# Strassen sums of the FFN's second product put together by adding transfers

## The chip, the cores and the metric

The kernel runs on one core of one Trainium2 chip. The metric is the device time of one execution in microseconds (us). The kernel before took 2555.97 us, the median of three runs (2553.58 to 2556.56). A change of 0.2%, about 5.1 us, is roughly what a measurement of this kernel can tell from none.

The engines have short names here: PE is TensorE, PEld its weight loads, DVE is VectorE, ACT is ScalarE, POOL is GpSimd and SP is SyncE, which issues transfers.

## The reference

Four layers, each a token mixer (latent attention, retention, gated linear attention, latent attention) and then an FFN, on 512 tokens of width 1024, all in float32. Only the FFN is touched:

```python
D_MODEL, SEQ, DEPTH = 1024, 512, 4
FFN_HIDDEN = 2816

def swiglu_ffn(x, w_in, w_out):
    gate, up = jnp.split(x @ w_in, 2, axis=-1)
    return (jax.nn.silu(gate) * up) @ w_out

# per layer, after the mixer:
x = layer_norm(DEEPNORM_ALPHA * x + swiglu_ffn(x, ffn_w_in[i], ffn_w_out[i]), ln_g[i, 1], ln_b[i, 1])
```

## The kernel before

Every product of two float32 matrices is made of three matmuls. An operand is split into a high part, rounded by an ACT cast, and a low part, the rest, subtracted on DVE (`split`, L100 to L103); `mm3` (L124) then multiplies high by high, high by low and low by high. Weights take this path: a transfer issued by SP fills a buffer `wraw` (three of them, 512 KB each), ACT writes `whi`, DVE writes `wlo` (six of each), and PE reads these two. A slot of `whi` and `wlo` comes free when the matmuls on it are done.

**The FFN.** The hidden width is cut into 22 blocks of 128, counted by f. For each f there are two projections, gate and up, of 24 matmuls each over `xh` and `xl` (tokens in 512 columns). ACT takes the silu of the gate, DVE multiplies it with the up part. For the blocks 0 to 15 the second product, with `w_out`, is done by a Strassen scheme. Two blocks, f even and f odd, make a pair. The product of the pair goes into one tile `ft` with room for seven 128x256 factors. Two of its four halves come with the even block and two with the odd one (DVE, L322). Then POOL makes the remaining factors with four adds and subtracts (L325 to L328), ACT casts all seven to `fh` and DVE subtracts the rest into `fl`. There is a single `ft`, so the next pair's first multiply waits until `fl` is done.

**The seven products.** Two pairs, four blocks of f, make a group, and `ffn_out` returns seven steps for it: p1, p5, p6, p2, p3, p7, p4. The four quarters of the weights' rows are called by the diff b11, b12, b21 and b22 (a 128 x 2 x 512 tile, 512 KB, each). Each step splits one tile of weights and runs 12 matmuls on it. The results are added from PSUM to the residual `xt` or to a tile `u`. The steps of a group run after the projections of the four blocks that follow it, two after each of the first three and one after the last (from f = 16 on they are spread over the blocks to 21). There are four groups per layer, 16 in all.

**The weights' sums before.** p1 loads b11 into a `wraw` buffer and b12 and b22 into two of the three buffers `wt`; p6 loads b21 into the third. Four DVE subtractions (L387) per group overwrite these buffers in place: b12-b11 for p5, b22 minus that for p6, b21 minus that for p4, b22-b12 for p7.

**The order.** A scheduler places the instructions: each engine runs its own list strictly in order, and an instruction whose semaphores are not up holds back all that stand behind it on its engine. This goes for SP and POOL too, whose lists also hold the transfers that they issue.

Of the kernel before, what the change touches and what calls it, by code (L numbers as in the profile page):

```python
# [9 lines left out]
F32 = mybir.dt.float32  # L10
# [3 lines left out]
ALU = mybir.AluOpType  # L14
AX = mybir.AxisListType

P = 128
# [5 lines left out]
ALPHA = (2.0 * DEPTH) ** 0.25  # L23
# [27 lines left out]
class Trunk:  # L51
# [121 lines left out]
        nc.sync.dma_start(self.bb, self.ins["ln_b"][i, k].partition_broadcast(P))  # L173
        self.stats = [self.small(12, "lnst") for _ in range(NT)]

    def acc(self, t, half, ps, coef, last):
        nc = self.nc
        x = self.xt[t][:, half * 512 : half * 512 + 512]
        if coef is None:
            nc.vector.tensor_tensor(x, ps, x, op=ALU.add)  # L180
        else:
            nc.vector.scalar_tensor_tensor(x, x, coef, ps, op0=ALU.mult, op1=ALU.add)
        if last:
            nc.vector.bn_stats(self.stats[t][:, half * 6 : half * 6 + 6], x)

# [110 lines left out]
    def ffn(self, l, out=None):  # L296
        nc = self.nc
        w_in, w_out = self.ins["ffn_w_in"][l], self.ins["ffn_w_out"][l]
        ns = 16
        self.fact, hs = {}, {}  # L300
        self.u = self.b((P, 2, 512), tag="u", name="u")
        half = lambda a: a.rearrange("p (a n) -> p a n", a=2)

        def evac(f, pg, pu):
            s = self.b()
            nc.scalar.activation(s, pg, AF.Silu)
            if f >= ns:
                if f < NF - 2:
                    if f % 2 == 0:
                        self.hp = self.b((P, 2, 512), F32R, "hh", "fh"), self.b((P, 2, 512), F32R, "hl", "fh")  # L310
                    h = tuple(x[:, f % 2, :] for x in self.hp)
                else:
                    h = self.bpair()
                nc.vector.tensor_tensor(s, pu, s, op=ALU.mult)
                self.split(h[0], h[1], s)
                hs[f] = h
                return
            if f % 2 == 0:
                self.ft = self.b((P, 7, 256), tag="ft", name="ft")
            ft = self.ft  # L320

            nc.vector.tensor_tensor(ft[:, 2:4, :] if f % 2 else ft[:, 1::-1, :], half(pu), half(s), op=ALU.mult)  # L322
            if f % 2:
                tt = nc.gpsimd.tensor_tensor
                tt(ft[:, 4, :], ft[:, 0, :], ft[:, 3, :], op=ALU.add)  # L325
                tt(ft[:, 5, :], ft[:, 4, :], ft[:, 1, :], op=ALU.subtract)
                tt(ft[:, 0, :], ft[:, 1, :], ft[:, 0, :], op=ALU.subtract)
                tt(ft[:, 6, :], ft[:, 2, :], ft[:, 5, :], op=ALU.subtract)  # L328
                h = self.b((P, 7, 256), F32R, "fh", "fh"), self.b((P, 7, 256), F32R, "fl", "fh")
                self.split(h[0], h[1], ft)  # L330
                self.fact[f // 2] = h

        nh = 3
        first = []
        for f in range(nh):
            wg = self.wcols(w_in, 0, KT, f * P, P)
            wu = self.wcols(w_in, 0, KT, F + f * P, P)
            first.append((wg, self.ps()))
            first.append((wu, self.ps()))
        for t0 in (0, 2):  # L340
            for n, (w2, ps) in enumerate(first):
                self.proj_f(w2, ps[:, t0 * P : (t0 + 2) * P], KT, lambda k: self.xm(k, t0, t0 + 2))
                if n % 2:
                    self.flush(2 + n // 2)
        for f in range(nh):
            evac(f, first[2 * f][1], first[2 * f + 1][1])
        rot = False
        todo = []
        for f in range(nh, NF):
            if f == nh + 1:  # L350
                rot = self.before(l + 1, nc.vector)
            if f == NF - 4 and rot:
                self.rope_sin()
            wg = self.wcols(w_in, 0, KT, f * P, P)
            pg = self.ps()
            self.proj_f(wg, pg, KT, self.xm)
            wu = self.wcols(w_in, 0, KT, F + f * P, P)
            pu = self.ps()
            self.proj_f(wu, pu, KT, self.xm)
            evac(f, pg, pu)  # L360
            if 4 <= f < ns + 4 and f % 4 == 0:
                c = f // 4 - 1
                todo = self.ffn_out(w_out, 2 * c, 2, c == 0)
            left = (4 - f % 4) if f < ns else NF - f
            for _ in range(-(-len(todo) // left) if todo else 0):
                todo.pop(0)()
        for tt in range(2):
            for hf, c in ((0, 1), (1, 0), (1, 1)):
                x = self.xt[2 * hf + tt][:, c * 512 : c * 512 + 512]
                nc.vector.tensor_tensor(x, x, self.u[:, tt, :], op=ALU.add)  # L370
        self.ln_begin(l, 1)
        st = lambda f, t: tuple(x[:, t * P : (t + 1) * P] for x in hs[ns + f])
        self.out_proj(st, w_out[ns * P :], NF - ns, None, True, out)

    def ffn_out(self, w, g0, n, begin):


        nc = self.nc
        rows = w[2 * g0 * P : 2 * (g0 + n) * P, :].rearrange("(g a p) c -> a p g c", a=2, p=P)
        B = {}  # L380

        def load(name, a, c, t):
            nc.sync.dma_start(t, rows[a][:, :, c * 512 : c * 512 + 512])
            B[name] = t

        wt = lambda: self.b((P, n, 512), name="wt", tag="t")
        sub = lambda to, x, y: nc.vector.tensor_tensor(B[to], B[x], B[y], op=ALU.subtract)  # L387

        def product(name, slot, to, u=None):

            hi, lo = self.wsplit(B[name], n, 512)
            ps = [self.ps() for _ in range(2)]
            for tt in range(2):
                for i in range(n):
                    s2 = tuple(x[:, slot, tt * P : (tt + 1) * P] for x in self.fact[g0 + i])
                    self.mm3(ps[tt], s2, (hi[:, i, :], lo[:, i, :]), i == 0, i == n - 1)
                for hf, c, first in to:
                    self.acc(2 * hf + tt, c, ps[tt], ALPHA if first else None, False)
                if u is not None:
                    x = self.u[:, tt, :]  # L400
                    if u:
                        nc.scalar.copy(x, ps[tt])
                    else:
                        nc.vector.tensor_tensor(x, ps[tt], x, op=ALU.add)

        s3, a11, a12, a22, s1, s2, s4 = range(7)

        def p1():
            load("1", 0, 0, self.wp.tile([P, n, 512], F32, tag="wraw", name="wraw", bufs=self.nraw))
            load("2", 0, 1, wt())  # L410
            load("3", 1, 1, wt())
            product("1", a11, [(0, 0, begin)], begin)

        def p5():
            sub("1", "2", "1")
            product("1", s1, [(0, 1, begin), (1, 1, begin)])

        def p6():
            sub("1", "3", "1")
            load("4", 1, 0, wt())  # L420
            product("1", s2, [], False)

        def p2():
            product("4", a12, [(0, 0, False)])

        def p3():
            sub("4", "4", "1")
            sub("2", "3", "2")
            product("3", s4, [(0, 1, False)])

        def p7():
            product("2", s3, [(1, 0, begin), (1, 1, False)])

        def p4():
            product("4", a22, [(1, 0, False)])

        return [p1, p5, p6, p2, p3, p7, p4]

    def load_x(self, x):

# [856 lines left out]
```

## Time and profile before

| | before |
|---|---|
| median of three runs | 2555.97 us |
| the profiled execution | 2556.05 us |
| its span, first to last instruction | 2554.2 us |
| PE busy in the span | 2524.5 us (99%) |
| DVE busy | 1776.7 us (70%) |
| ACT busy | 976.8 us (38%) |
| POOL busy | 212.4 us (8%) |
| mean granted clock of TensorE | 0.998 |
| DMA | 232.36 MB, 29.9% of the 16 engines' time |

The profile is of one execution, 1.9 us longer than its span and within 0.1 us of the median. A busy time is the time in which an engine has at least one instruction running. PE's matmuls overlap, so a matmul that is listed with 389 ns can follow the one before it after 226 ns: the rate is read from counts in a stretch, not from durations. The FFN stages lie at about 212 to 590, 1036 to 1372, 1640 to 1970 and 2190 to 2554 us.

### The profile page before, as it was taken

Reading aid. Unit: us, or ns where it says so; the run is one execution under the profiler, and the core shown is the slowest. Engines: PE = TensorE matmul, PEld = TensorE weight load, DVE = VectorE, ACT = ScalarE, POOL = GpSimd, SP = SyncE. Lnnn points to the kernel's source line nnn. Section 1 sums busy time; section 2 is a strip of 40 time slices with the busy share of each in tenths; the row PEclk is TensorE's granted clock in tenths of the full one; section 3 lists DMA queues with packets and bytes.
Section 4 is the critical chain, followed back from the end, with each engine's and each line's share of the span. In section 5 each row is a group of like instructions: output and inputs, shape, how many; then the busy total and the mean of one; then the engine's idle time right before and its main releaser. Section 6 shows DMA issues by size and latency. Waiting matters only on the chain.

```text
span 2554.2 us, 32600 instructions
## 1 busy us (share of the span) xinstructions
PE 2524.5 (99%) x12804; PEld 2147.2 (84%) x12804; DVE 1776.7 (70%) x2980; ACT 976.8 (38%) x1405; POOL 212.4 (8%) x279
## 2 busy tenths in 40 slices
PE   8999999999999999999999999999999999999998
PEld 7788888888888888988888899988888788988887
DVE  6887766658655647666657878966657686666656
ACT  4653333323342323333332665233332564233331
POOL 3000111000101101111100000011100200011101
PEclk9999999999999999999999999999999999999999
DMA  4213333323222333333333322333332311333331
GB/s 149 75 42 95 99 102 105 99 83 100 76 90 66 95 96 99 99 99 99 107 99 82 91 74 75 112 99 99 99 91 79 91 58 57 109 99 99 99 91 58
DMA packets 294714, 232.36 MB, mean 91 GB/s; under 512 B 21120, under 2 KB 244480, under 8 KB 294560
## 3 DMA queue, kind: packets, MB, share of 16 engines
q1 hardware_dynamic: 294560, 230.28, 29.9%
q8 instruction: 100, 1.64, 0.3%
q14 instruction: 54, 0.44, 0.1%
HBM read 228.15 MB, written 2.10 MB: 90 GB/s over the span
## 4 chain that ended last, share of the span: by engine, by line
PE 93%; DVE 3%; ACT 2%; DMA 1%; issue 1%; POOL 1%; SPq 0%; DVEq 0%; ACTq 0%; POOLq 0%
PE ps L126 30%; PE ps L127 30%; PE ps L128 30%; PE tp L659 1%; PE tp L156 1%; DVE wlo L102 1%; PE ps L640 1%; PE ps L639 0%; ACT whi L101 0%; DMA wraw<-in_mla_w_ukv 0%; DMA wraw<-in_mla_w_down 0%; DMA wraw<-in_ret_w_in 0%; ACT bh L101 0%; ACT b L549 0%; PE tp L903 0%
## 5 line engine op out<-in xcount | busy, mean ns | idle before, releaser
L101 ACT CAST whi<-wraw 128x1024 fp32r<-128x1024 f32 (+3 forms) x398 | 411.9, 1040 | 699.0 <-PE ps L127 234.1
L126 PE MATMUL ps<-xh,whi 128*128 128x512 f32 (+1 forms) x1792 | 656.8, 367 | 0.0
L127 PE MATMUL ps<-xl,whi 128*128 128x512 f32 (+1 forms) x1792 | 656.5, 366 | 0.1
L128 PE MATMUL ps<-xh,wlo 128*128 128x512 f32 (+1 forms) x1792 | 656.4, 366 | 0.0
L102 DVE TENSOR_TENSOR wlo<-wraw,whi 128x1024 fp32r<-128x1024 f32 (+3 forms) x398 | 487.6, 1234 | 212.5 <-ACT whi L101 205.1
L128 PEld LDWEIGHTS ps<-xh,wlo 128*128 128x128 f32 x1792 | 337.9, 189 | 55.0
L127 PEld LDWEIGHTS ps<-xl,whi 128*128 128x128 f32 x1792 | 337.9, 189 | 54.9 <-DVE lnx L139 0.3
L126 PEld LDWEIGHTS ps<-xh,whi 128*128 128x128 f32 x1792 | 337.6, 189 | 55.3 <-issue 0.4
L126 PE MATMUL ps<-whi,xh 128*128 128x512 f32 (+3 forms) x752 | 264.5, 352 | 0.7 <-ACT xh L101 0.7
L128 PE MATMUL ps<-whi,xl 128*128 128x512 f32 (+3 forms) x752 | 262.6, 349 | 2.3 <-DVE xl L102 2.3
L127 PE MATMUL ps<-wlo,xh 128*128 128x512 f32 (+3 forms) x752 | 262.3, 349 | 0.1
L180 DVE TENSOR_TENSOR xt<-ps,xt 128x512 f32<-128x512 f32 x288 | 187.2, 682 | 34.9 <-PE ps L128 34.9
L126 PE MATMUL ps<-whi,fh 128*128 128x512 f32 x448 | 174.3, 389 | 0.0
L127 PE MATMUL ps<-wlo,fh 128*128 128x512 f32 x448 | 174.3, 389 | 0.0
L128 PE MATMUL ps<-whi,fl 128*128 128x512 f32 x448 | 174.3, 389 | 0.0
L128 PEld LDWEIGHTS ps<-whi,xl 128*128 128x128 f32 x752 | 142.7, 190 | 20.2 <-DVE xl L102 3.3
L126 PEld LDWEIGHTS ps<-whi,xh 128*128 128x128 f32 x752 | 142.8, 190 | 18.3 <-ACT xh L101 1.1
L127 PEld LDWEIGHTS ps<-wlo,xh 128*128 128x128 f32 x752 | 142.9, 190 | 17.1 <-DVE wlo L102 0.7
L325 POOL TENSOR_TENSOR ft<-ft 128x256 f32<-128x256 f32 x32 | 24.6, 770 | 1466.9 <-DVE ft L322 1466.9
L322 DVE TENSOR_TENSOR ft<-ps,b 128x512 f32<-128x512 f32 x64 | 44.2, 690 | 139.6 <-PE ps L128 76.1
L101 ACT CAST whi<-wt 128x1024 fp32r<-128x1024 f32 x64 | 67.5, 1054 | 190.3 <-PE ps L127 133.4
L126 PE MATMUL ps<-bh 128*128 128x256 f32 (+1 forms) x376 | 123.8, 334 | 6.7 <-ACT bh L101 6.4
(258 smaller groups left out, 3941.3 us busy)
## 6 DMA issues: line engine op xcount, KB each, us to landing
wraw<-in_ffn_w_in SPq DMA_DIRECT2D x176, 512.0 KB, 3.9
wt<-in_ffn_w_out SPq DMA_DIRECT2D x48, 512.0 KB, 4.8
wraw<-in_ret_w_in SPq DMA_DIRECT2D x48, 512.0 KB, 3.9
wraw<-in_ffn_w_out SPq DMA_DIRECT2D x40, 512.0 KB, 3.3
wraw<-in_gla_w_in SPq DMA_DIRECT2D x22, 512.0 KB, 3.6
wraw<-in_mla_w_o SPq DMA_DIRECT2D x16, 512.0 KB, 3.7
wraw<-in_ret_w_o SPq DMA_DIRECT2D x16, 512.0 KB, 4.6
wraw<-in_mla_w_down SPq DMA_DIRECT2D x8, 512.0 KB, 4.6
```

The source lines that it names most:

```text
L101: a = self.nc.scalar.copy(hi, src)
L102: b = self.nc.vector.tensor_tensor(lo, src, hi.bitcast(F32), op=ALU.subtract)
L126: mm(out, s[0], m[0], start=start, stop=False)
L127: mm(out, s[0], m[1], start=False, stop=False)
L128: mm(out, s[1], m[0], start=False, stop=stop)
L156: nc.tensor.transpose(ps[:, j, :], self.xt[t][:, (4 * g + j) * P : (4 * g + j + 1) * P], self.ident)
L180: nc.vector.tensor_tensor(x, ps, x, op=ALU.add)
L322: nc.vector.tensor_tensor(ft[:, 2:4, :] if f % 2 else ft[:, 1::-1, :], half(pu), half(s), op=ALU.mult)
L325: tt(ft[:, 4, :], ft[:, 0, :], ft[:, 3, :], op=ALU.add)
L640: nc.tensor.matmul(ps, qr[:, sl], krz[e], start=False, stop=True)
L659: nc.tensor.transpose(ps[:, kk, qq, :], pq[qq][:, k * P : (k + 1) * P], self.ident)
```

## The change

The Strassen sums of the weights are no longer differences made by DVE. They become plain sums, b12+b11, b22+b12+b11, b12+b22 and b21+b22+b12+b11. Each is put together in one `wt` buffer: SP transfers the first quarter into it, and then POOL issues one more transfer for each further quarter, which adds its elements to what lies there (`accum_op`). One buffer's transfers follow each other, each waiting until the one before has landed. The minus signs move to the other operand (two of POOL's four instructions swap add for subtract) and to the output (one result, and `u` in two of its three uses, are subtracted). Quarters that stand alone (b11, b21, b22) are loaded into `wraw` for their own product. Per group there are 7 loads by SP instead of 4, 7 adding transfers by POOL instead of none, and no L387.

```diff
-    def acc(self, t, half, ps, coef, last):
+    def acc(self, t, half, ps, coef, last, minus=False):
...
+        op = ALU.subtract if minus else ALU.add
+        if coef is not None:
+            nc.vector.scalar_tensor_tensor(x, x, coef, ps, op0=ALU.mult, op1=op)
+        elif minus:
+            nc.vector.tensor_tensor(x, x, ps, op=op)
         else:
-            nc.vector.scalar_tensor_tensor(x, x, coef, ps, op0=ALU.mult, op1=ALU.add)
+            nc.vector.tensor_tensor(x, ps, x, op=op)
...
-                tt(ft[:, 4, :], ft[:, 0, :], ft[:, 3, :], op=ALU.add)
+                tt(ft[:, 4, :], ft[:, 0, :], ft[:, 3, :], op=ALU.subtract)
                 tt(ft[:, 5, :], ft[:, 4, :], ft[:, 1, :], op=ALU.subtract)
                 tt(ft[:, 0, :], ft[:, 1, :], ft[:, 0, :], op=ALU.subtract)
-                tt(ft[:, 6, :], ft[:, 2, :], ft[:, 5, :], op=ALU.subtract)
+                tt(ft[:, 6, :], ft[:, 2, :], ft[:, 5, :], op=ALU.add)
...
-                nc.vector.tensor_tensor(x, x, self.u[:, tt, :], op=ALU.add)
+                nc.vector.tensor_tensor(x, x, self.u[:, tt, :], op=ALU.subtract if c else ALU.add)
...
-        def load(name, a, c, t):
-            nc.sync.dma_start(t, rows[a][:, :, c * 512 : c * 512 + 512])
-            B[name] = t
-
-        wt = lambda: self.b((P, n, 512), name="wt", tag="t")
-        sub = lambda to, x, y: nc.vector.tensor_tensor(B[to], B[x], B[y], op=ALU.subtract)
...
+        block = lambda ac: rows[ac // 2][:, :, ac % 2 * 512 : ac % 2 * 512 + 512]
+
+        def load(blocks):
+            if len(blocks) == 1:
+                t = self.wp.tile([P, n, 512], F32, tag="wraw", name="wraw", bufs=self.nraw)
+            else:
+                t = self.b((P, n, 512), name="wt", tag="t")
+            nc.sync.dma_start(t, block(blocks[0]))
+            for ac in blocks[1:]:
+                nc.gpsimd.dma_start(t, block(ac), accum_op=ALU.add)
+            return t
...
-            hi, lo = self.wsplit(B[name], n, 512)
+            hi, lo = self.wsplit(load(blocks), n, 512)
...
-        def p5():
-            sub("1", "2", "1")
-            product("1", s1, [(0, 1, begin), (1, 1, begin)])
-
-        def p6():
-            sub("1", "3", "1")
-            load("4", 1, 0, wt())
-            product("1", s2, [], False)
...
-        def p3():
-            sub("4", "4", "1")
-            sub("2", "3", "2")
-            product("3", s4, [(0, 1, False)])
...
+        return [
+            lambda: product([b11], a11, [(0, 0, begin, False)], begin),
+            lambda: product([b12, b11], s1, [(0, 1, begin, False), (1, 1, begin, False)]),
+            lambda: product([b22, b12, b11], s2, [], False),
+            lambda: product([b21], a12, [(0, 0, False, False)]),
+            lambda: product([b22], s4, [(0, 1, False, False)]),
+            lambda: product([b12, b22], s3, [(1, 0, begin, False), (1, 1, False, True)]),
+            lambda: product([b21, b22, b12, b11], a22, [(1, 0, False, False)]),
+        ]
```

The lists of PE and ACT hold the same operations in the same order as before. DVE's list loses the 64 L387. POOL's list gains 112 adding transfers. Its list before, from the first FFN's first pair on (`ft_2894` is the pair of blocks 0 and 1, `ft_2909` of 2 and 3, `ft_3082` of 4 and 5; the waits name the engine or transfer semaphore):

```order
L325 TENSOR_TENSOR ft_2894<-ft_2894 128x256 [waits DVE_49]
L326 TENSOR_TENSOR ft_2894<-ft_2894 128x256 [waits Pool_49]
L327 TENSOR_TENSOR ft_2894<-ft_2894 128x256
L328 TENSOR_TENSOR ft_2894<-ft_2894 128x256 [waits Pool_49]
L325 TENSOR_TENSOR ft_2909<-ft_2909 128x256 [waits DVE_49]
L326 TENSOR_TENSOR ft_2909<-ft_2909 128x256 [waits Pool_49]
```

The same place on POOL after the change (`wt_3438` is the buffer of the first group's p4, the sum of four quarters, and `wt_3553` that of the next group's p5; `DMAHW` is a transfer issued by SP, `DMASW` one issued by POOL):

```order
L331 TENSOR_TENSOR ft_2894<-ft_2894 128x256 [waits Pool_49]
L394 DMA wt_3438<-in_ffn_w_out 128x2x512 [waits DMAHW3_49,DMASW0_49,DVE_49]
L394 DMA wt_3438<-in_ffn_w_out 128x2x512 [waits DMASW4_49]
L328 TENSOR_TENSOR ft_2909<-ft_2909 128x256 [waits DVE_49,Pool_49]
L329 TENSOR_TENSOR ft_2909<-ft_2909 128x256 [waits Pool_49]
L330 TENSOR_TENSOR ft_2909<-ft_2909 128x256
L331 TENSOR_TENSOR ft_2909<-ft_2909 128x256 [waits Pool_49]
L394 DMA wt_3438<-in_ffn_w_out 128x2x512 [waits DMASW5_49]
L394 DMA wt_3553<-in_ffn_w_out 128x2x512 [waits DMAHW6_49,DMASW3_49,DVE_49]
L328 TENSOR_TENSOR ft_3082<-ft_3082 128x256 [waits DVE_49,Pool_49]
```

Two adding transfers of p4's sum now stand between the factors of the first and the second pair, and the second of them waits for the first. The first group of each of the four layers has this order; in the other groups only the first adding transfer stands ahead of the group's second pair.

DVE's list at the same place, before (`wraw_3084` holds b11 and then, in place, the sums for p5 and p6):

```order
L102 TENSOR_TENSOR wlo_3091<-wraw_3084,whi_3090 128x1024
L322 TENSOR_TENSOR ft_2909<-ps_2575,b_2907 128x2x256
L387 TENSOR_TENSOR wraw_3084<-wt_3086,wraw_3084 128x1024
L387 TENSOR_TENSOR wt_3086<-wt_3088,wt_3086 128x1024
L102 TENSOR_TENSOR wlo_3114<-wraw_3084,whi_3113 128x1024
L387 TENSOR_TENSOR wraw_3084<-wt_3088,wraw_3084 128x1024
```

and after (`wt_3108` is the buffer of p5's sum):

```order
L102 TENSOR_TENSOR wlo_3087<-wraw_3084,whi_3086 128x1024
L325 TENSOR_TENSOR ft_2909<-ps_2575,b_2907 128x2x256
L102 TENSOR_TENSOR wlo_3112<-wt_3108,whi_3111 128x1024
L102 TENSOR_TENSOR wlo_3136<-wraw_3133,whi_3135 128x1024
L325 TENSOR_TENSOR ft_2909<-ps_2948,b_2973 128x512
```

The low part of p5's weights, after which p5's buffer is free for p4's sum, moved up to the place of the first L387.

## Rows read from the trace of the kernel before

**Rows 1.** Stretch 300 to 400 us: busy time and instructions of each engine, clock, DMA.

```profile
300.00:400.00 100.00, 100.00 (x443) 82.80 (x442) 67.03 (x72) 34.58 (x36) 11.21 (x12) 1.00 0.37 110
```

**Rows 2.** Instructions of line L387: count, min/median/max ns, first and last start; who waited.

```profile
L387 DVE TENSOR_TENSOR wraw<-wt,wraw x32: 1212/1224/1228, 282.4 to 2422.7; 128x1024 f32<-128x1024 f32 x32
...
L387 DVE TENSOR_TENSOR wt<-wt x16: 1224/1226/1227, 283.6 to 2419.5; 128x1024 f32<-128x1024 f32 x16
L387 DVE TENSOR_TENSOR wt<-wt,wraw x16: 1215/1218/1226, 302.5 to 2449.4; 128x1024 f32<-128x1024 f32 x16
...
  ACT whi L101: 14.9, 4
```

**Rows 3.** Second pair, first FFN, POOL: start, length in us, line, tiles.

```profile
289.77 0.74 POOL L325 TENSOR_TENSOR ft<-ft 128x256 f32<-128x256 f32 x1 [12.85 <-DVE ft L322]
290.59 1.60 POOL L326 TENSOR_TENSOR ft<-ft 128x256 f32<-128x256 f32 x1
```

**Rows 4.** The same pair on ACT and DVE, then PE's first use; same columns.

```profile
293.62 1.70 ACT L101 CAST fh<-ft 128x1792 fp32r<-128x1792 f32 x1 [3.82 <-POOL ft L328]
...
295.35 2.03 DVE L102 TENSOR_TENSOR fl<-ft,fh 128x1792 fp32r<-128x1792 f32 x1 [3.76 <-ACT fh L101]
...
299.61 0.39 PE L126 MATMUL ps<-whi,fh 128*128 128x512 f32 x1
...
300.52 0.39 PE L127 MATMUL ps<-wlo,fh 128*128 128x512 f32 x1
300.75 0.39 PE L128 MATMUL ps<-whi,fl 128*128 128x512 f32 x1
```

**Rows 5.** Ahead of that, first FFN: cast of p1's weights on ACT, then DVE.

```profile
279.04 1.04 ACT L101 CAST whi<-wraw 128x1024 fp32r<-128x1024 f32 x1
...
280.63 1.22 DVE L102 TENSOR_TENSOR wlo<-wraw,whi 128x1024 fp32r<-128x1024 f32 x1
281.76 0.68 DVE L322 TENSOR_TENSOR ft<-ps,b 128x512 f32<-128x512 f32 x1
282.36 1.21 DVE L387 TENSOR_TENSOR wraw<-wt,wraw 128x1024 f32<-128x1024 f32 x1
```

**Rows 6.** DMA queues of the whole kernel, from the page: packets, MB, share of engines.

```profile
q1 hardware_dynamic: 294560, 230.28, 29.9%
```

**Rows 7.** Issues in 312 to 313.5, 1109 to 1111, 1001 to 1003: us to landing.

```profile
wt<-in_ffn_w_out SPq DMA_DIRECT2D x1, 512.0 KB, 3.4
...
wt<-in_ffn_w_out SPq DMA_DIRECT2D x1, 512.0 KB, 5.3
...
DMA to landing us min/median/max: 6.6/7.3/8.0
```

**Rows 8.** Second pair in the third FFN: DVE and PE.

```profile
1672.66 2.03 DVE L102 TENSOR_TENSOR fl<-ft,fh 128x1792 fp32r<-128x1792 f32 x1 [4.57 <-ACT fh L101]
...
1676.24 0.39 PE L126 MATMUL ps<-whi,fh 128*128 128x512 f32 x1
```

**Rows 9.** Third group, first FFN: p5's weights, the second pair, PE's use of it.

```profile
406.80 1.23 DVE L102 TENSOR_TENSOR wlo<-wraw,whi 128x1024 fp32r<-128x1024 f32 x1 [0.66 <-ACT whi L101]
...
412.17 0.74 POOL L325 TENSOR_TENSOR ft<-ft 128x256 f32<-128x256 f32 x1 [28.82 <-DVE ft L322]
...
417.76 2.02 DVE L102 TENSOR_TENSOR fl<-ft,fh 128x1792 fp32r<-128x1792 f32 x1 [2.56 <-ACT fh L101]
...
425.64 0.39 PE L127 MATMUL ps<-wlo,fh 128*128 128x512 f32 x1
```

**Rows 10.** The longest pause of PE in the first layer, and the stretch around it.

```profile
47.26 0.69 PE L532 MATMUL tp<-ident,b 128*128 128x128 f32 x2 [4.36 <-DVE b L526]
...
45.00:52.00 7.00, 4.74 (x12) 3.79 (x13) 2.88 (x5) 1.27 (x2) 0.60 (x2) 0.52 0.61 195
```

More of the change, by code (lines that the diff above doesn't have):

```diff
@@ L174, in ln_begin @@
         self.stats = [self.small(12, "lnst") for _ in range(NT)]
-    def acc(self, t, half, ps, coef, last):
+    def acc(self, t, half, ps, coef, last, minus=False):
         nc = self.nc
         x = self.xt[t][:, half * 512 : half * 512 + 512]
-        if coef is None:
-            nc.vector.tensor_tensor(x, ps, x, op=ALU.add)
+        op = ALU.subtract if minus else ALU.add
[3 more added lines that the diff above has]
+            nc.vector.tensor_tensor(x, x, ps, op=op)
         else:
-            nc.vector.scalar_tensor_tensor(x, x, coef, ps, op0=ALU.mult, op1=ALU.add)
+            nc.vector.tensor_tensor(x, ps, x, op=op)
         if last:
@@ L379, in ffn_out, with product @@
         rows = w[2 * g0 * P : 2 * (g0 + n) * P, :].rearrange("(g a p) c -> a p g c", a=2, p=P)
-        B = {}
-        def load(name, a, c, t):
-            nc.sync.dma_start(t, rows[a][:, :, c * 512 : c * 512 + 512])
-            B[name] = t
-        wt = lambda: self.b((P, n, 512), name="wt", tag="t")
-        sub = lambda to, x, y: nc.vector.tensor_tensor(B[to], B[x], B[y], op=ALU.subtract)
-        def product(name, slot, to, u=None):
-            hi, lo = self.wsplit(B[name], n, 512)
+        block = lambda ac: rows[ac // 2][:, :, ac % 2 * 512 : ac % 2 * 512 + 512]
[8 more added lines that the diff above has]
+            return t
+        def product(blocks, slot, to, u=None):
+            hi, lo = self.wsplit(load(blocks), n, 512)
             ps = [self.ps() for _ in range(2)]
@@ L396, in product @@
                     self.mm3(ps[tt], s2, (hi[:, i, :], lo[:, i, :]), i == 0, i == n - 1)
-                for hf, c, first in to:
-                    self.acc(2 * hf + tt, c, ps[tt], ALPHA if first else None, False)
+                for hf, c, first, minus in to:
+                    self.acc(2 * hf + tt, c, ps[tt], ALPHA if first else None, False, minus)
                 if u is not None:
@@ L406, in ffn_out @@
         s3, a11, a12, a22, s1, s2, s4 = range(7)
[L408 to L412, printed above, removed]
-        def p5():
-            sub("1", "2", "1")
-            product("1", s1, [(0, 1, begin), (1, 1, begin)])
-        def p6():
-            sub("1", "3", "1")
-            load("4", 1, 0, wt())
-            product("1", s2, [], False)
-        def p2():
-            product("4", a12, [(0, 0, False)])
-        def p3():
-            sub("4", "4", "1")
-            sub("2", "3", "2")
-            product("3", s4, [(0, 1, False)])
[L431 to L437, printed above, removed]
+        b11, b12, b21, b22 = range(4)
+        return [
[7 more added lines that the diff above has]
+        ]
     def load_x(self, x):
```

## The prediction

> **What bounds the kernel now.** I read the page's busy times first, then the stretches of the FFN, then PE's waits there, and last the places where the changed instructions stand. In an undisturbed stretch of an FFN PE is busy for all of its 100 us and starts 443 matmuls at the full clock, one every 226 ns [rows 1]. In the waits of PE and of its weight loads over the whole first FFN there is no entry at all. So in the part that the change touches PE is fed without a pause, and DVE, with 67 of 100 us, and POOL, with 11, have room. What DVE is freed of can shorten nothing there unless something had waited for it. The FFN only gets longer, and by just what is missing when PE wants it.
>
> **What is removed.** 64 subtractions of 1.22 us, 78 us of DVE [rows 2]. Their only follower with a wait is ACT, four times, 14.9 us in all: the cast of p5's weights in the first group of each layer. PE reads these weights some 17 us later, so this wait is covered. Worth: nothing. The sign swaps keep the form and size of their instructions: nothing.
>
> **What is added.** 112 adding transfers on POOL and 48 more loads on SP. With 512 KB each that is 160 x 0.524 = 84 MB on top of 230 [rows 6]. The engines of the transfers were busy for 37% of a stretch at 110 GB/s [rows 1]. The new traffic falls in about 62 us per group, 10 x 0.524 MB or 84 GB/s, so the share rises to some 65%, and to 90% if an add costs double. Loads get slower, up to the 7 to 8 us of three at once [rows 7], but weights are split five tiles ahead of PE, some 20 us, so this is covered too.
>
> What is not covered is the order on POOL. An adding transfer waits at the head of POOL's list, and the four instructions that make a pair's factors stand behind it; behind these wait ACT's cast `fh`, DVE's `fl`, and PE. I go through it for the first group of the first layer.
>
> - *When the buffer is free.* p4's sum reuses p5's buffer. p5's sum has long been loaded, so its cast follows that of p1's weights on ACT, at about 280.1, and its low part takes the place of the first L387 on DVE, after the multiply that ends at 282.4 [rows 5]. It ends at 283.6.
> - *First load.* SP issues it then. One load alone landed after 3.4 us and the second of two close ones after 5.3 [rows 7]. p2's load goes out some 1.8 us earlier, when p1's low part is done [rows 5], so I take 4.6, between the two: 288.2.
> - *First add.* No row shows a transfer issued by POOL or one that adds: all packets of the program are on SP's queue [rows 6]. From below it is a plain load, 3.4 us. From above I take 8.0, the longest of three at once [rows 7]. An add has to fetch the new elements and the old ones, so the row that it is nearest to is the two close loads, 5.3, and POOL must first write its instructions out: I take 6.5 from issue to landing, so 294.7.
> - *Second add.* It waits for that landing, and POOL's next instruction waits until it is issued: between nothing and the longest POOL instruction here, 1.6 us [rows 3]. I take 1.0, so the factors start at 295.7 where they started at 289.8 [rows 3]: 5.9 us late.
> - *What of it is covered.* `fl` ended at 297.4, and PE loads its first part with the matmul at 300.52 [rows 4]. That is 3.1 us of slack, and 5.9 - 3.1 = 2.8 us are PE's pause. DVE's multiply for the next block and the low part of p6's weights are queued behind `fl` and come late too, but PE wants the banks and weights that they release only after p1 and p5, over 4 us later: no second pause.
>
> The other layers have the same order. In the third FFN `fl` ended at 1674.7 and PE's load of it is at 1676.24 + 0.9 = 1677.1, so the slack is 2.4 and the pause 3.5 [rows 8]. The sum is 3 x 2.8 + 3.5 = 11.9 us.
>
> In the later groups only the first add of p4's sum stands ahead of the second pair. In the third group the buffer comes free at 408.0, the load lands 4.6 us later, the add is issued by 413.6, and the factors start 1.4 us late with 425.6 - 419.8 = 5.8 us of slack [rows 9]: covered, even with the load at 8.0. The second and third add come after the pair's factors and have over 20 us before the next pair. p4's sum, loaded once and added to three times, needs 4.6 + 3 x 7.5 = 27 us and has 44 before its split. All these are free as long as an add takes under some 13 us.
>
> **One rule against the trace.** A load of 512 KB alone took 3.4 us here [rows 7]. The Trainium skill, "DMA: Bandwidth & Descriptors", in the section "Anatomy of one DMA — SWDGE (gpsimd) path", gives 2.0 us plus the bytes at 436 GB/s, which is 3.2 us, so the trace agrees; and the Trainium skill, "Collectives: The Full Stack", in the section on the bandwidth ceiling (the fold count and why AG ≠ RS ≠ AR), says that a transfer that adds reads two sources and so runs at half the rate of a copy, while the add itself costs nothing. No run so far shows it for an add into SBUF. As an estimate from the two pages an add is 2.0 + 2.4 = 4.4 us, and the sum by that would be 288.2 + 4.4 + 1.0 - 289.8 - 3.1 = 0.7 us per layer, 1.4 in the third FFN, 3.5 us in all: 2559.6, no change that can be measured.
>
> **The rivals.**
> - *Covered after all: no change.* If the first add and the issue of the second take at most 5.6 us together, the four pauses stay under 5.1 us; up to 4.7 us they vanish. For it speaks that a plain load takes 3.4. Against it: the software issue counts twice and the add moves twice the bytes. The time is 2556 to 2561. The estimate from the two pages of the Trainium skill above falls in this case.
> - *Slower transfers and a cold clock: clearly worse than forecast.* With 5.3 for the load, 8.0 for the add and 1.6 for the issue the factors start at 298.5, and PE pauses 5.6 us, or 23 over the four layers. After a pause of 4.4 us PE was granted 0.52 of its clock for 7 us, so it ran at the lower of its two levels, 1.2 GHz, and lost about 7.0 x 0.48 = 3.4 us [rows 10]; four times that is 14. Together 37 us: 2593. An add of 12 us gives 9 + 3.4 per layer, 2606, and from 13 us on the later groups stall too.
> - *Faster.* DVE's freed time would have to reach PE. That needs pauses of PE in the FFNs that go away, and there are none [rows 1]; I see no path to 5 us.
> - *The sums are not overlapped at all:* the scheduler puts the adds late, and each p7 and p4 waits for its chain. The lists say otherwise: the loads and adds stand a whole group ahead.
>
> **How the numbers follow.** The sum is made against the profiled execution, 2556.05 us, which is the median within 0.1. Forecast: 2556.05 + 11.9 = 2568 us. Chances: the forecast, pauses between 1.3 and 6 us per layer, 58%; no change 27%; clearly worse 12%; faster 3%. A change under 0.2%, 5.1 us, is what a measurement here can't tell from none. The range has to reach down to the covered case, with the 2 us by which runs of this kernel differ, and up to the bound of the costs, 2593: 2554 to 2593. That leaves out the slowest adds and half of the faster case. Faster by over 0.2%: 0.03; within: 0.27; slower: 0.70.
>
> **What would show it.** Right: PE waits for `fl` of the second pair, once per layer, close to p1's first matmuls, and no other wait over 1 us in the FFNs; POOL's factors of that pair start 5 to 7 us later after DVE's multiply than before, behind an adding transfer; the second pairs of the later groups start 1 to 2 us late and nobody waits. Adding transfers land after 5 to 8 us. Wrong: adds that land under 4.5 us (no pause), or over 13 (pauses in every group, casts of `wt` waiting for transfers); PE waiting for `whi` of a `wt` tile; a lower granted clock after the pauses with pauses under 4 us; matmuls that start more than 226 ns apart in undisturbed stretches.

## The result and the profile after

The changed kernel took 2577.86 us, the median of four runs (2576.12 to 2579.98), against 2556.26 us (2553.58 to 2557.67) of the kernel before in the same comparison. The ratio is 1.0086, with a 95% interval of 1.0073 to 1.0098: slower by 21.6 us. The forecast, 2568.0, had the sign, the mechanism of about three quarters of the loss, and only about half of its size.

The page of the kernel after, busy times, DMA queues and the issues that matter (KB of one, median us from issue to landing):

```profile
PE 2532.7 (98%) x12804; PEld 2151.5 (84%) x12804; DVE 1686.1 (65%) x2916; ACT 975.2 (38%) x1405; POOL 337.4 (13%) x391
...
q1 hardware_dynamic: 307616, 255.44, 32.7%
q0 software_dynamic: 30464, 58.73, 14.2%
...
wraw<-in_ffn_w_in SPq DMA_DIRECT2D x176, 512.0 KB, 4.9
wt<-in_ffn_w_out POOLq DMA_DIRECT2D x112, 512.0 KB, 5.9
```

DVE is freed of 91 us, POOL gets 125 us, and a second queue, that of POOL, moves 58.7 MB beside the one of [rows 6], which got 25 MB more. The answer to [rows 1] is a stretch of the first FFN behind its start (busy us and instructions of each engine, clock, DMA share, GB/s):

```profile
310.00:410.00 100.00, 100.00 (x443) 82.81 (x442) 57.78 (x65) 32.44 (x33) 23.13 (x23) 1.00 0.77 182
```

PE starts 443 matmuls here as before, though the DMA share rose from 0.37 to 0.77. So the traffic as such slows nothing in the middle of an FFN; what was lost must lie at single places. PE's waits over the whole span name them (us in total, times, longest); none of these three stands in the list of the kernel before:

```profile
PE ps L126 <- ACT fh L101: 5.9, 3, 4.0
PE tp L156 <- DVE xt L207: 5.2, 2, 4.2
PE ps L128 <- DVE fl L102: 4.8, 4, 1.3
```

**The second pair of the first group.** The first FFN on POOL, which answers [rows 3]: the first add of p4's sum, the second, and the first of the four instructions that make the factors:

```profile
289.13 1.21 POOL L394 DMA_DIRECT2D wt<-in_ffn_w_out  x1 [11.60 <-DVE ft L325]
295.33 1.21 POOL L394 DMA_DIRECT2D wt<-in_ffn_w_out  x1 [4.99 <-DMA wt<-in_ffn_w_out]
296.09 1.23 POOL L328 TENSOR_TENSOR ft<-ft 128x256 f32<-128x256 f32 x1
```

And behind them, which answers [rows 4], ACT's cast, DVE's low part, and PE's first matmuls on either:

```profile
299.56 1.68 ACT L101 CAST fh<-ft 128x1792 fp32r<-128x1792 f32 x1 [10.55 <-POOL ft L331]
...
301.28 2.02 DVE L102 TENSOR_TENSOR fl<-ft,fh 128x1792 fp32r<-128x1792 f32 x1 [11.01 <-ACT fh L101]
...
301.30 0.50 PE L126 MATMUL ps<-whi,fh 128*128 128x512 f32 x1 [1.63 <-ACT fh L101]
...
303.36 0.50 PE L128 MATMUL ps<-whi,fl 128*128 128x512 f32 x1 [1.32 <-DVE fl L102]
```

**Ahead of the FFN of the second layer** lies a wait that the prediction does not have. The fourth add of the first group goes out on POOL; then come ACT's cast of the FFN's first weights, which waits for their load, DVE's low part of it, and the layer norm behind it on DVE's list, on which PE's transposes wait:

```profile
1024.31 1.21 POOL L394 DMA_DIRECT2D wt<-in_ffn_w_out  x1 [4.84 <-issue]
1030.47 1.20 POOL L394 DMA_DIRECT2D wt<-in_ffn_w_out  x1 [4.95 <-issue]
...
1039.53 1.05 ACT L101 CAST whi<-wraw 128x1024 fp32r<-128x1024 f32 x1 [5.34 <-DMA wraw<-in_ffn_w_in]
...
1040.61 1.22 DVE L102 TENSOR_TENSOR wlo<-wraw,whi 128x1024 fp32r<-128x1024 f32 x1 [4.12 <-ACT whi L101]
...
1043.34 1.41 DVE L207 SCALAR_TENSOR_TENSOR xt<-xt,lny,ln_b 128x512 f32<-128x512 f32 x2
...
1044.23 0.85 PE L156 MATMUL tp<-ident,xt 128*128 128x128 f32 x4 [4.25 <-DVE xt L207]
```

The add of 1030.47 and the load that SP issued at 1031.17, from issue to landing:

```profile
wt<-in_ffn_w_out POOLq DMA_DIRECT2D x1, 512.0 KB, 8.6
wraw<-in_ffn_w_in SPq DMA_DIRECT2D x1, 512.0 KB, 8.3
```

The same load took 3.7 us in the kernel before. The two met: the add took 8.6 us instead of 5.8, the load 8.3 instead of 3.7. The Trainium skill, "DMA: Bandwidth & Descriptors", in the section "Issuing engines are not separate DMA queues", says that transfers run on the same DMA engines whichever engine issued them, and mix with each other; the trace agrees.

**The clock.** Three stretches behind such waits (first FFN, ahead of the second, third FFN); the column before the DMA share is the granted clock:

```profile
303.80:307.20 3.40, 3.40 (x10) 2.65 (x9) 3.40 (x5) 0.77 (x1) 0.00 (x0) 0.50 1.01 211
1044.50:1047.90 3.40, 3.40 (x19) 3.40 (x18) 1.63 (x3) 1.17 (x2) 0.00 (x0) 0.50 0.57 199
1693.03:1699.86 6.83, 5.17 (x11) 3.64 (x12) 6.03 (x6) 3.66 (x5) 1.22 (x1) 0.50 0.60 116
```

PE ran at 0.50, the lower of its two levels, 1.2 GHz. Each stretch costs half of the time in which PE was busy in it: 1.7, 1.7 and 2.6 us.

**The bill.** ACT's list holds the same operations in the same order in both kernels, so the start of one and the same cast of weights in the two timelines gives how late the kernel after is at that point:

| the same cast, before | after | late by | what lies between it and the row above |
|---|---|---|---|
| 263.51 | 262.72 | -0.8 | start, first mixer |
| 326.84 | 331.17 | 4.3 | second pair, first FFN: 5.1 |
| 1021.53 | 1025.57 | 4.0 | |
| 1044.88 | 1054.68 | 9.8 | ahead of the second FFN: 5.8 |
| 1091.89 | 1103.79 | 11.9 | second pair, second FFN: 2.1 |
| 1665.37 | 1678.12 | 12.75 | ahead of the third FFN: 0.9 |
| 1681.92 | 1702.42 | 20.5 | second pair, third FFN: 7.75 |
| 2240.81 | 2261.24 | 20.4 | |
| 2257.36 | 2279.68 | 22.3 | second pair, fourth FFN: 1.9 |

The four second pairs make 16.9 us, the two places ahead of the FFNs 6.7, the other rows -1.2: 22.4, the difference of the two spans (2576.6 - 2554.2).

### The profile page after: what moved, and what is told of

Same layout as the page of the kernel before. It is cut to its first block, busy times and chain, and to the rows that moved or that the text cites. A ratio compares the mean times of both kernels' runs of the same rounds, so it can differ in the third digit from the quotient of the medians.

```text
span 2576.6 us, 32896 instructions
## 1 busy us (share of the span) xinstructions
PE 2532.7 (98%) x12804; PEld 2151.5 (84%) x12804; DVE 1686.1 (65%) x2916; ACT 975.2 (38%) x1405; POOL 337.4 (13%) x391
## 3 DMA queue, kind: packets, MB, share of 16 engines
q0 software_dynamic: 30464, 58.73, 14.2%
## 4 chain that ended last, share of the span: by engine, by line
PE 89%; DVE 4%; DMA 2%; ACT 2%; issue 1%; POOL 1%; DVEq 0%; SPq 0%; POOLq 0%; ACTq 0%
PE ps L126 29%; PE ps L128 28%; PE ps L127 28%; PE tp L647 1%; PE tp L156 1%; DVE wlo L102 1%; DMA wraw<-in_ffn_w_in 1%; DMA wt<-in_ffn_w_out 1%; PE ps L628 1%; PE ps L627 0%; ACT whi L101 0%; POOL wt L394 0%; DVE xt L206 0%; DMA wraw<-in_mla_w_ukv 0%; DMA wraw<-in_ret_w_in 0%
## 5 line engine op out<-in xcount | busy, mean ns | idle before, releaser
L102 DVE TENSOR_TENSOR wlo<-wraw,whi 128x1024 fp32r<-128x1024 f32 (+3 forms) x398 | 480.2, 1213 | 249.2 <-ACT whi L101 242.0
L394 POOL DMA_DIRECT2D wt<-in_ffn_w_out x112 | 136.5, 1219 | 1193.8 <-DVE lnst L187 337.5
L185 DVE TENSOR_TENSOR xt<-ps,xt 128x512 f32<-128x512 f32 x256 | 169.6, 684 | 35.2 <-PE ps L128 34.8
L102 DVE TENSOR_TENSOR fl<-ft,fh 128x1792 fp32r<-128x1792 f32 x32 | 64.8, 2025 | 140.6 <-ACT fh L101 140.6
```

What stands on the lines that cost most here:

```text
L102: b = self.nc.vector.tensor_tensor(lo, src, hi.bitcast(F32), op=ALU.subtract)
L185: nc.vector.tensor_tensor(x, ps, x, op=op)
L394: nc.gpsimd.dma_start(t, block(ac), accum_op=ALU.add)
```

## The experiments

**Theory A**: the cost is one of order and of one meeting: factors that stand behind an adding transfer on POOL (some 17 us), and an add that meets the FFN's first loads (some 7). **Theory B**: it is the 84 MB more traffic, or the loads, signs and DVE work changed along with it. All comparisons are with the kernel before (2555.99 us in the first four, 2556.51 in the others). What an edit gives back is 21.6 us less what it is still slower by.

### All adds left out

```diff
-            for ac in blocks[1:]:
+            for ac in []:
```

> All 112 adding transfers are left out; the 48 more loads by SP, the new signs and the missing DVE subtractions stay (the sums are not put together, so the weights of p5, p6, p7 and p4 are only their first quarter). Both theories below say that the time comes from the adding transfers: 2555 to 2558 us, no pause of PE at the second pair and no wait at the transposes ahead of the FFN of the second layer. If the 48 loads, the signs or the freed DVE cost the 21 us instead, 2570 to 2578 remain.

Measured: 2556.37 us, ratio 1.0001 (0.9992 to 1.0010). No wait for `fh`, `fl` or the norm at L207 is left in PE's list. So the whole 21.6 us hang on the adding transfers. And with the 48 more loads and some 75 us less on DVE the time is that of the kernel before: neither costs nor gains anything.

### One add instead of three for p4's first sum

```diff
-            for ac in blocks[1:]:
+            for ac in blocks[1:2] if begin and len(blocks) == 4 else blocks[1:]:
```

> In the first group of each layer p4's sum gets one adding transfer instead of three (its second and third are left out, 8 of 112 in all). Theory A, the order on POOL: the factors of the second pair stood behind the second add, which waits for the landing of the first. Now they stand behind one issue of 1.2 us only, so the pauses at the second pair go in all four layers, and with them the 4.3 + 2.1 + 7.4 + 1.9 = 15.7 us that ACT's casts drifted there: about 2562 us, with the wait at the transposes ahead of the FFNs left over. Theory B, the traffic of the transfers as such: 104 of 112 adds are still there, so 2575 to 2578.

Measured: 2560.42 us, ratio 1.0019 (1.0010 to 1.0029): 4.4 us are left, so 8 adds of 112 carried 17.2. No wait for `fh` or `fl` is left in PE's list; the norm's is (the profiled execution took 2564.71 us; the ten lie between 2558.28 and 2569.14):

```profile
PE tp L156 <- DVE xt L207: 5.3, 2, 4.5
```

By the casts of the bill this profile loses nothing at the four second pairs, 6.0 us ahead of the second FFN and 1.1 ahead of the third. Theory B would have kept 2575. What costs here is not the add but what stands behind its landing on POOL.

### No add for p7's first sum

```diff
-            for ac in blocks[1:]:
+            for ac in [] if begin and blocks == [b12, b22] else blocks[1:]:
```

> In the first group of each layer p7's sum gets no adding transfer (4 of 112 left out; it is the last of the four that go out ahead of the FFN). Theory A: this add went out 0.7 us before the FFN's first loads of the second layer and made them land 4.6 us later (8.3 instead of 3.7), and through ACT's cast, DVE's low part and the layer norm behind it PE waited 4.2 us and then ran 3.4 us at half the clock. Without it 5.8 us go in the second layer and up to 1 in the third: about 2571 us, with the pauses at the second pair left as they are. Rival: the norm is late because of all four adds or of the loads of SP, and taking one away changes less than 2 us: 2576 to 2578.

Measured: 2570.29 us, ratio 1.0058 (1.0041 to 1.0074): 14.3 us are left, 7.3 gone. The mirror of the one before: the norm's wait is gone, those at the second pairs are there.

```profile
PE ps L128 <- DVE fl L102: 5.3, 4, 1.3
...
PE ps L126 <- ACT fh L101: 2.8, 3, 2.0
```

By the casts of the bill nothing is lost ahead of the second FFN any more (5.8 in the change) and 0.25 us ahead of the third (0.9). But the second pairs lose 11.8 us in this profile, not 16.9, though this edit doesn't touch them, so not all of the 7.3 us are the meeting's.

### The factors on DVE

```diff
-                tt = nc.gpsimd.tensor_tensor
+                tt = nc.vector.tensor_tensor
```

> Nothing is left out: the four instructions that make a pair's factors are issued on DVE instead of POOL, for all 32 pairs, so that nothing but the adding transfers stands on POOL in the FFNs. Theory A: the factors no longer wait for any transfer, the four pauses at the second pair go, and the wait ahead of the FFNs stays: about 2562 us. DVE gets some 32 x 4 x 0.35 = 45 us more and has room. Theory B, traffic: 2575 to 2578. A third case: DVE's list is now longer at the pair and fl comes late itself, with new waits of PE for fl.

Measured: 2562.08 us, ratio 1.0025 (1.0016 to 1.0035). All adds and all sums are there, and 15.5 us are gone; no wait of PE for `fh` or `fl` is left. DVE's busy time rose from 1686.1 to 1725.7 us, and PE's only new wait on it is 0.4 us, once. The wait ahead of the FFNs stays, shorter in this profile:

```profile
PE tp L156 <- DVE xt L207: 2.0, 2, 1.5
```

That wait is not all of the 6.1 us that are left. This profile is 6.2 us longer than that of before: 1.5 us are lost ahead of the second FFN, 1.4 ahead of the third, none at a second pair, and the rest inside the mixers, which this edit doesn't touch; where it comes from is not shown.

### Plain transfers instead of adding ones

```diff
-                nc.gpsimd.dma_start(t, block(ac), accum_op=ALU.add)
+                nc.gpsimd.dma_start(t, block(ac))
```

> The 112 transfers issued by POOL stay, with the same bytes, buffers and waits, but overwrite instead of adding (the sums are not put together: p5, p6, p7 and p4 use the last quarter that is loaded). In the changed kernel an add landed a median of 5.9 us after its issue and the next one, also into another buffer, went out 0.3 us after that landing. Theory A: reading the old elements is a part of the price; a plain one lands after about 4.6 us (3.4 of a load by SP and 1.2 for the writing of the instructions), the factors of the second pair start 1.2 us earlier in each layer, and the four adds ahead of the FFN are done before its first loads: 2560 to 2566 us. Rival: what costs is the issue by software, adding is free; plain ones land after 5.8 us too and the time stays at 2575 to 2578.

Measured: 2558.63 us, ratio 1.0007 (0.9998 to 1.0016), better than either side expected. The four transfers ahead of the second FFN on POOL, and the page's rows of POOL's queue and of its issues:

```profile
1006.89 0.76 POOL L394 DMA_DIRECT2D wt<-in_ffn_w_out  x1 [19.90 <-PE ps L128]
1008.17 0.72 POOL L394 DMA_DIRECT2D wt<-in_ffn_w_out  x1 [0.53 <-issue]
1009.48 0.73 POOL L394 DMA_DIRECT2D wt<-in_ffn_w_out  x1 [0.58 <-issue]
1013.72 0.72 POOL L394 DMA_DIRECT2D wt<-in_ffn_w_out  x1 [3.51 <-DMA wt<-in_ffn_w_out]
...
q0 software_dynamic: 16128, 58.73, 6.9%
...
wt<-in_ffn_w_out POOLq DMA_DIRECT2D x112, 512.0 KB, 4.0
```

A plain transfer occupies POOL for 0.73 us instead of 1.21, lands after 4.0 us (3.7 to 3.8 with nothing beside it) instead of 5.9, and three of them are under way together. So the issue by software is not what costs; the adding is: 2 us to landing and half a microsecond on POOL. The DMA engines tell it too: for the same 58.73 MB POOL's queue takes 6.9% of their time here and 14.2% with adds, twice as much. With the adding away both stalls nearly vanish, on the same order of instructions. How much of that is the shorter landing and how much the going out together, this run doesn't separate.

### Adds cut in halves

```diff
-                nc.gpsimd.dma_start(t, block(ac), accum_op=ALU.add)
+                for i in range(n):
+                    nc.gpsimd.dma_start(t[:, i, :], block(ac)[:, i, :], accum_op=ALU.add)
```

> Each adding transfer is cut into two of half the size, 224 in all, with the same bytes and result. The second half waits for nothing that the first one does. If POOL holds an adding transfer back until the one before it has landed, the second half goes out some 0.3 us after the first has landed, and a pair of halves takes twice a fixed part more than one whole; if it is held by its own waits alone, the second goes out right after the first's issue, under 1.5 us later. With 3.4 us of fixed cost and 2.4 us for the bytes of a whole add, a half lands after about 4.6 us, and held back one after the other the sums get 3.7 us longer per add, the factors of the second pair stand behind two or three of them, and the time rises to 2590 us or more; not held back it stays within 5 us of 2577.

Measured: 2592.68 us, ratio 1.0142 (1.0123 to 1.0160). The time is that of the first case, but its reason is wrong. The first adds of the kernel on POOL (three issues in a row, then one):

```profile
222.25 2.85 POOL L395 DMA_DIRECT2D wt<-in_ffn_w_out  x3 [165.36 <-DVE lnst L187]
227.39 0.88 POOL L395 DMA_DIRECT2D wt<-in_ffn_w_out  x1 [2.29 <-issue]
```

Three halves went out one after the other and the fourth 0.3 us after the first had landed (222.25 + 4.9). Whole adds never did so: of the 111 that follow another one in the changed kernel, none started before that one had landed, those into other buffers included (1024.31 and 1030.47 above, "issue"). So how much may be under way together depends on the size, and adds count for more than plain transfers of the same bytes; what sets the limit these runs don't show. The time rose through the order again: more adds that wait for landings stand ahead of the second pair's factors, one even among them, and PE waits for them in all four layers:

```profile
PE ps L126 <- ACT fh L101: 18.9, 4, 5.5
```

Ahead of the FFN no wait is left: the shorter adds are done in time.

### p4's adds behind the factors

```diff
-                tt(ft[:, 6, :], ft[:, 2, :], ft[:, 5, :], op=ALU.add)
+                self.made[f // 2] = tt(ft[:, 6, :], ft[:, 2, :], ft[:, 5, :], op=ALU.add).ins
...
-                nc.gpsimd.dma_start(t, block(ac), accum_op=ALU.add)
+                with self.tc.issue_after(self.made[1]) if begin and len(blocks) == 4 else nullcontext():
+                    nc.gpsimd.dma_start(t, block(ac), accum_op=ALU.add)
```

(`made[1]` is the last instruction of the second pair's factors, `made[0]` of the first's; only POOL's list changes.)

> Nothing is left out and all 112 adds stay: in the first group of each layer the three adds of p4's sum stand behind the second pair's factors on POOL, instead of two of them ahead. Theory A, the order on POOL: the pauses at the second pair go as they did with one add, 2560 to 2562 us, with the wait ahead of the FFNs left (5.8 us in the second layer, 1 in the third). p4's sum is ready some 10 us later and PE wants it over 20 us after that. Theory B, the transfers as such: 2575 to 2578.

Measured: 2559.46 us, ratio 1.0014 (1.0005 to 1.0023), just under what theory A expected. The same 112 adds, the same bytes, no wait for `fh` or `fl` left, and some 18.6 us of 21.6 are gone: the 17 of the second pairs, which hung on the place in POOL's list alone, and a part of the rest, since the longer of the two waits at the norm is only 1.6 us in this profile. Here the fourth add went out 1.9 us ahead of the FFN's first load, not 0.7, and that load took 5.7 us instead of 8.3; in the run with one add for p4 it was 0.65 us and 8.5, in the one with the factors on DVE 1.7 us and 5.6, and where the add was done or left out, 3.7. A meeting shifted by a microsecond thus decides over some 4 us, and no edit here set that distance. The 112 adds of the changed kernel show the same dependence: the 31 beside which SP issued a load of weights between 0.35 us ahead and 0.8 us behind took 7.5 to 10.0 us, the six with no load under way 5.75 to 5.84.

### p4's and p7's adds behind the factors

```diff
-                nc.gpsimd.dma_start(t, block(ac), accum_op=ALU.add)
+                after = self.made.get({b21: 1, b12: 0}[blocks[0]] if begin and blocks in ([b21, b22, b12, b11], [b12, b22]) else None)
+                with self.tc.issue_after(after) if after else nullcontext():
+                    nc.gpsimd.dma_start(t, block(ac), accum_op=ALU.add)
```

> As the kernel before this one, and the first group's p7 add stands behind the first pair's factors on POOL instead of ahead of the FFN. Nothing is left out and all 112 adds stay. If the order on POOL and the one add that meets the FFN's first loads are the whole of the 21 us, it takes 2555 to 2557.5 us, no change against the kernel before. If traffic or the loads cost something of their own, 2559 or more.

Measured: 2556.29 us, ratio 1.0001 (0.9992 to 1.0010). With all sums, adds and bytes of the change it is as fast as the kernel before, and no faster. The two places of theory A are the whole of the loss. No wait for `fh`, `fl` or the norm is left in PE's list, which begins as that of the kernel before:

```profile
PE ps L126 <- ACT bh L101: 5.9, 7, 1.5
PE tp L520 <- DVE b L514: 4.8, 2, 4.4
```

## Why the prediction was half right

**Removed work is worth nothing: right.** DVE lost 91 us and no kernel became faster; the one without adds is at 1.0001.

**Later groups and traffic inside the FFN: right.** PE has no wait there, at a DMA share of 0.77 (forecast: some 0.65, and 90% if an add costs double, which by its own numbers, 17 x 0.524 MB in 62 us, is 85%). An add did cost the DMA engines double: 14.2% of their time against 6.9% for the same bytes. In the third group [rows 9] the factors started at 417.95 where the kernel, 4.3 us late as a whole by then, would have had them at 416.5: 1.4 us late, as said, and nobody waits.

**The chain on POOL: right**, each step to within 0.7 us, for the first FFN:

| step | forecast | measured |
|---|---|---|
| buffer free | 283.6 | 284.2 |
| first load | 4.6, to 288.2 | 4.2, landed 288.5 |
| until the add is issued | 0 | 0.7, at 289.1 |
| first add | 6.5 (3.4 to 8.0), to 294.7 | 5.8, landed 294.9 |
| second add's issue | 1.0, to 295.7 | 0.4 + 0.8, factors at 296.1 |
| `fl` late | 5.9 | 301.28 - 295.35 = 5.9 |

That the 5.9 came out to the tenth is luck: the factors started 6.3 us late (296.09 against 289.77), the steps being off in both directions, and they then took 0.4 us less than before.

The add's size came out between the forecast and the estimate that the prediction worked out from two pages of the Trainium skill. A plain transfer by POOL took 3.7 to 3.8 us here, an add 5.8 when it had nothing beside it. These pages of the Trainium skill, "DMA: Bandwidth & Descriptors" ("Anatomy of one DMA — SWDGE (gpsimd) path") and "Collectives: The Full Stack" ("The bandwidth ceiling: the fold count and why AG ≠ RS ≠ AR"), gave 3.2 for a plain transfer and an estimate of 4.4 for an adding one. The first is said of transfers that POOL issues, and the prediction held it against one of SP's (3.4); POOL's own took 3.7 to 3.8. The half rate that the second page of the Trainium skill gives shows in the DMA engines' time, 14.2% against 6.9%, so there the trace agrees; but from issue to landing an adding transfer costs 2.0 us more than a plain one where the estimate has 1.2 more; the measurements decide. The covered case, which followed from the 4.4, did not come.

**The pauses: mis-sized.** Forecast 2.8, 2.8, 3.5 and 2.8, sum 11.9; measured 5.1, 2.1, 7.75 and 1.9, sum 16.9. Three terms:

- *The clock* stood in the rival of slower transfers alone, after pauses of over 4 us. In the first FFN waits of 1.6 and 1.3 us with one short run of matmuls between them were followed by 3.4 us at half the clock, 1.7 us lost; in the third it is 2.6. That is 4.3 of the 5 us that the sum is short. After 0.2 and 1.3 us in the second FFN and 1.3 in the fourth the clock stayed. The prediction named a lower clock after pauses under 4 us as what would prove it wrong, and this came. Its price in the rival was too high: it halved all 7.0 us of the stretch in [rows 10], of which PE was busy for 4.74, so 2.3 us were lost there and not 3.4.
- *The third FFN* had the least slack, as said, and there the first add met a load of `w_in` as well, issued 0.7 us behind it: 7.8 us instead of 5.8. (In the first FFN such a load came 1.2 us behind, and the add took 5.8.)

```profile
1679.74 1.22 POOL L394 DMA_DIRECT2D wt<-in_ffn_w_out  x1 [12.56 <-DVE ft L325]
1687.95 1.20 POOL L394 DMA_DIRECT2D wt<-in_ffn_w_out  x1 [6.99 <-DMA wt<-in_ffn_w_out]
...
1693.85 0.80 PE L126 MATMUL ps<-whi,fh 128*128 128x512 f32 x1 [4.03 <-ACT fh L101]
...
1695.91 0.79 PE L128 MATMUL ps<-whi,fl 128*128 128x512 f32 x1 [0.83 <-DVE fl L102]
```

- *PE's own time*: it reached p1 of the first FFN 0.8 us earlier than in the trace of before (298.8 instead of 299.6), while the buffer came free 0.6 us later than forecast. The slack is a difference of two chains that shift against each other from run to run: without p7's add, on the same order at this place, PE waited 0.2 and 1.3 us here, the clock stayed, and the first FFN lost 2.1 us, not 5.1.

In the second and the fourth FFN the pauses came out shorter than forecast, by 0.7 and 0.9 us, which hides a part of these terms in the sum.

**What the prediction never looked at: 7 us.** It followed the first group's p4 and the later groups, and called all other adds free as long as one takes under 13 us. But the adds of the first group's p5, p6 and p7 go out ahead of the FFN, in the last part of the mixer, and whole adds go one after the other: the four in the second layer, some 6.1 us each while undisturbed, last from 1012.2 to 1039.1. The last of them reaches the FFN's first loads, and there is no weight in store yet: the first cast waits, DVE's low part behind it, the layer norm behind that, and PE. The step of the prediction that failed is "weights are split five tiles ahead of PE, some 20 us, so this is covered too": true in the middle of an FFN, not at its start. There the load landed 8.3 us after its issue, PE waited 4.2 us and then lost 1.7 to the clock. The prediction looked at no place outside the FFNs for who stands behind a weight load there.

The size of the whole fell between the forecast and the rival of slower transfers (2593), whose clock was right and whose add of 8.0 was not, except where a load met it.

## What to carry to other kernels

A transfer issued from a computing engine's list is an instruction with a wait: look at what stands behind it there, and put chains that wait for their own landings behind the work that someone else needs. When a change adds transfers, go to the places where the store of weights is empty (the start of a stage), not to the mean share of the DMA engines: that rose to 0.77 inside an FFN here without a trace in PE. And a pause that is cut in two can still cost the clock, so add half of the stretch behind it to the sum.

## What was not expected of the hardware

- An adding transfer of 512 KB into SBUF landed 5.8 us after its issue with nothing beside it and kept POOL for 1.21 us; a plain one 3.7 to 3.8 and 0.73.
- For the same 58.73 MB POOL's queue took 14.2% of the DMA engines' time with adds and 6.9% with plain transfers.
- Whole adds were never under way together, not even into different buffers; up to three plain ones or three halves were.
- An add and a load of the same size, issued 0.7 us apart, took 8.6 and 8.3 us. With 1.7 to 1.9 us between them the load took 5.6 to 5.7, alone 3.7. The 31 adds with such a load between 0.35 us ahead and 0.8 us behind took 7.5 to 10.0.
- The granted clock fell to 0.50 for 3.4 us after two waits of 1.6 and 1.3 us with 0.7 us of matmuls between them, and for 6.8 us around waits of 4.0 and 0.8.
